# Attention's products with the values: from two split passes of 128 columns to plain fp32 at two places of 64 columns

## The chip, the cores and the metric

The kernel runs on one core of a Trainium2 chip. Its five engines work side by side, each through its own queue in order: the tensor engine (PE, with the loads of its weights shown as PEld), the vector engine (DVE), the scalar engine (ACT), GpSimd (POOL) and SyncE (SP), which issues most transfers. The metric is the device time of one execution in microseconds; the median of three runs counts.

## What is computed

One inference step of a decoder layer for a prompt of 1024 tokens and 8 single tokens ("samples") that share the weights: a half-step feed-forward block, one input projection, an attention part with 8 heads (MLA) beside an mLSTM part with 4 heads, one output projection, a second feed-forward block, a per-layer embedding and a final norm, all in fp32. The change is in the attention of the prompt, which the reference writes as follows:

```python
k_nope = (ckv @ w_uk).reshape(B, S, H, NOPE_DIM)
v = (ckv @ w_uv).reshape(B, S, H, V_DIM)          # V_DIM = 64
...
s = (jnp.einsum('bqhd,bkhd->bhqk', qn_b, k_nope, ...)
     + jnp.einsum('bqhr,bkr->bhqk', qr_b, krope, ...)) * scale
s = jnp.where(kpos[None, :] <= qpos[:, None], s, -jnp.inf)
p = jax.nn.softmax(s, axis=-1)
return jnp.einsum('bhqk,bkhd->bqhd', p.astype(v.dtype), v)
```

## The kernel before

Activations lie with features on the 128 partitions and tokens along the free axis. Most products are made of three passes in the type fp32r: operands are split into a high part (a cast on ACT) and a low part (a subtraction of that cast on DVE or GpSimd), and high x high, high x low and low x high are added in PSUM (`split` L177, `mm3` L195 to L198).

The attention of the prompt runs over 16 items: 8 heads, each with two halves of 512 queries (`Q` = 0, 1). Two generators share the loop at L1362. `scores` (L1312, `att_s` L1144) makes, for one block of 128 queries at a time, the scores of all keys up to it (`pss`, three fp32r passes of up to 512 columns for each 512 keys, L1164 to L1166), the maximum on DVE (L1168, L1171), the exponential on ACT (L1176) and the normalisation by the sum on DVE or ACT (L1183, L1181); the result is a tile `P` with queries on partitions. It runs `LEAD` = 3 blocks ahead of the other generator, `att_pv` (L1187).

`att_pv` goes over key blocks of 128 keys, 4 of them for Q = 0 and 8 for Q = 1. For a key block, `tr` transposes the blocks of `P` (up to four, one for each query block, L1196) into a PSUM tile `pT`, and splits it into an fp32r tile `PT`, one buffer for each key block: cast on ACT (L178), subtraction on DVE (L182). Three key blocks later (`SKEW`) follow two passes into `po` (L1211): the weights are 128 columns of the value tile `vv`, high halves of 64 values beside low halves, and the moving operand is the high and then the low part of `PT`, up to 512 queries wide; the last four key blocks lie on the diagonal, where 384, 256 and 128 columns are left. Rows 0 to 63 of `po` hold what the high values give, rows 64 to 127 what the low values give; a copy on ACT (L1216) and an addition on DVE (L1217) bring them together in `aT`. The value tiles come from `v_all` (L964), eight of them, each split from PSUM by ACT and DVE (L974).

Between these units stand, at places fixed by the emitted microseconds of tensor work, steps of other generators: the attention of the samples over gathered cache pages (`ss` L1072 and `ol` L1118, plain fp32 products with 32 weight columns at four places of the array; the pages `kt` and `nt` come by indirect transfers from GpSimd's queue, L1049 and L1058), the projection of the embeddings (`pj`), and near the end the preparation of the output projection (`mx`, `hT`).

The order on PE and SP is the order in the source. The order on ACT, DVE and GpSimd is set by a scheduler when the program is built, and so is which of the 43 big buffers a tile gets. `PT`, `vv`, `P`, `kt`, `nt` and the weights all share these 43 buffers, and an instruction that fills one waits for the last reader of the tile that lay there.

Of the kernel before, what the change touches and what calls it, by code (L numbers as in the profile page):

```python
# [7 lines left out]
F32 = mybir.dt.float32  # L8
F32R = mybir.dt.float32r
I32 = mybir.dt.int32  # L10
AF = mybir.ActivationFunctionType
ALU = mybir.AluOpType
# [14 lines left out]
HEADS = 8  # L27
# [26 lines left out]
ACT_NORM = (1, 3, 5)  # L54
SKEW = 3
LEAD = 3
AHEAD = 4
# [33 lines left out]
class Emitter:  # L91
    """Orders what is emitted: a step can be put off until some microseconds of tensor work lie before it,
    and slow chains are taken step by step between the units of tensor work."""

# [37 lines left out]
def trunk(ctx: ExitStack, tc, I, O):  # L132
    nc = tc.nc
    pe, act, dve, pool, sp = nc.tensor, nc.scalar, nc.vector, nc.gpsimd, nc.sync
# [12 lines left out]
    def nm(p):  # L147
        uid[0] += 1
        return f"{p}_{uid[0]}"

    def B(shape, dt=F32, p="b"):
        t = big.tile(shape, dt, tag="b", name=nm(p))
        return t
# [9 lines left out]
    def TN(shape, dt=F32, p="t"):  # L163
        t = tin.tile(shape, dt, tag="t", name=nm(p))
        return t

    def PS(shape, p="ps"):
        t = psp.tile(shape, F32, tag="ps", name=nm(p))
        return t
# [7 lines left out]
    def split(hi, lo, src, eng=None):  # L177
        act.copy(hi, src)  # L178
        if eng is pool:
            pool.tensor_tensor(out=lo, in0=src, in1=hi.bitcast(F32), op=ALU.subtract)  # L180
        else:
            dve.tensor_tensor(out=lo, in0=src, in1=hi.bitcast(F32), op=ALU.subtract)  # L182
# [23 lines left out]
    class Acts:  # L206
        """Eight feature tiles, split, cut by token group: 15 of a group's 16 slices in five tiles of its own."""

# [74 lines left out]
    class Norm:  # L283
# [6 lines left out]
        def lift(self, g, k):  # L290
            """The group's slice k times its gain only: the group's scale is left to what follows the products."""
            x = SC(p="xf")
            dve.tensor_scalar(out=x, in0=self.h[k][:, GS[g]], scalar1=gc[:, self.g0 + k:self.g0 + k + 1], scalar2=None, op0=ALU.mult)
            hi, lo = self.x.outs(g, k, 1)[0]
            split(hi, lo, x, pool if k in LIFT_POOL else None)
# [13 lines left out]

    # the units of work of one weight tile over the token groups; the last group comes late at first  # L310
    def units(n, early):
# [7 lines left out]
    def ffn(h, nrm, wg, wu, wd, nxt, order, begin, mid, ahead, lat, aheads, late={}):  # L319
        """order: the first units; the last group's second half of the norm is put in after the first unit."""  # L320
        xn = nrm.x
# [99 lines left out]

    # ---- start
    ones = C([128, 128], name="ones")
# [3 lines left out]
    h = [B([128, T], F32, "h") for _ in range(KD)]  # L427
# [46 lines left out]

    # ---- constants of the mixing part
    ident = C([128, 128], name="ident")
# [12 lines left out]
    first = [(0, 0), (1, 0), (0, 1), (1, 1), (0, 2), (1, 2)]  # L489
# [15 lines left out]

    # ---- input projection
    zs = {}
# [42 lines left out]

    # ---- gates: rows of (head, chunk), the running maximum over the chunks, columns by a transpose
    def log_sigmoid(t, rows, n):
# [21 lines left out]
    def gates():  # L574
# [3 lines left out]
        for i in range(2):  # L578
            rows = slice(64 + 32 * i, 64 + 32 * i + MH)
# [49 lines left out]
        pool.dma_start(out=acb, in_=md3.partition_broadcast(128))  # L629
        # samples  # L630
        gs = TN([MH, 2, NB_S], p="gs")
# [19 lines left out]
        pool.dma_start(out=sgb, in_=sgd.partition_broadcast(128))  # L651
        # rotary key
        trig = B([64, T], F32, "trig")
# [11 lines left out]

    # ---- mLSTM of the prompt, a chunk a step
    xd = tc.dram_tile([MH, 128, NC, CH], F32, name="xd")
# [87 lines left out]

    # ---- norms of the latents
    cks = C([128, 2, NB_S], name="cks")
# [14 lines left out]

    # ---- one step of the mLSTM for the samples, a head at a time
    xs = C([128, MH * NB_S], name="xs")
# [61 lines left out]
    for n, (i, g) in enumerate(us):  # L836
# [3 lines left out]
        if n == 3:  # L840
            spill_h()
            h = None
# [3 lines left out]
        if i > 6 and g == 2 and i % 4 == 1 and i < 21:  # L846
            hd = (i - 9) // 4
# [14 lines left out]

    # ---- MLA projections, kept in DRAM until their head's turn
    vd = tc.dram_tile([8, 128, HEADS * 128], F32, name="vtd")
# [99 lines left out]
    def v_all(uvh, uvl):  # L964
        for kb in range(8):
            ps = PS([128, 512])
            t = slice(kb * 128, (kb + 1) * 128)
            for ct in range(2):
                mm3(ps, ck[ct][0][:, t], ck[ct][1][:, t], uvh[:, ct, :], uvl[:, ct, :], ct == 0, ct == 1)
            vv = B([128, HEADS, 128], F32R, "vv")  # L970
            split(vv[:, :, 0:64], vv[:, :, 64:128], ps.rearrange("p (h v) -> p h v", h=HEADS))
            vtok.append(vv)
            em.spend(1.3)
            yield  # L974
# [10 lines left out]
    vtok = []  # L985
# [29 lines left out]

    # ---- attention of the samples over their pages
    NI = NB_S * N_PAGES
# [8 lines left out]
    aT = [B([128, T], F32, "aT") for _ in range(4)]  # L1026
# [113 lines left out]

    # ---- attention of the prompt
    em.flush()
# [44 lines left out]
    def att_pv(hd, P, Q):  # L1187
        po = PS([128, 512], "po")
        nkb = 4 * Q + 4
        pxs = {}  # L1190

        def tr(kb):
            j0 = max(0, kb - 4 * Q)
            ps = PS([128, 4, 128], "pT")
            for j in range(j0, 4):
                pe.transpose(ps[:, j, :], P[j][:, kb * 128:(kb + 1) * 128], ident)  # L1196
            px = B([128, 2, 4, 128], F32R, "PT")
            split(px[:, 0, j0:4, :], px[:, 1, j0:4, :], ps[:, j0:4, :])
            pxs[kb] = px

        for kb in range(SKEW):
            tr(kb)
            yield
        for kb in range(nkb):
            if kb + SKEW < nkb:
                tr(kb + SKEW)
            yield
            j0 = max(0, kb - 4 * Q)
            px = pxs.pop(kb)
            for i in range(2):  # L1210
                pe.matmul(po[:, j0 * 128:512], vtok[kb][:, hd, :], px[:, i, j0:4, :].rearrange("p j q -> p (j q)"),  # L1211
                          start=(kb == 0 and i == 0), stop=(kb == nkb - 1 and i == 1))
            px = None
        r0 = 64 * (hd % 2)
        t = aT[hd // 2][r0:r0 + 64, 512 * Q:512 * Q + 512]
        act.copy(t, po[0:64])  # L1216
        dve.tensor_tensor(out=t, in0=po[64:128], in1=t, op=ALU.add)  # L1217
        yield
# [56 lines left out]

    # ---- output projection of the mixing part
    n2 = Norm(None, "xn", G_FF2)
    wo = {}

    h = []  # L1280
# [46 lines left out]
    for i in range(V_PRE):  # L1327
        next(vs, None)
    while done < 4 + LEAD:
        next(sc)  # L1330
# [31 lines left out]
    for n, (hd, Q) in enumerate(items):  # L1362
        pv = att_pv(hd, Ps.pop(n), Q)
        steps = SKEW + 1 + 4 * Q + 4
        left = len(items) - 1 - n
        for i, _ in enumerate(pv):
            em.spend(0.6)
            at(left, i)
            while done < 4 * (n + 1) + LEAD + 4 * (i + 1) / steps:
                next(sc)  # L1370
# [18 lines left out]
    aT = None  # L1389
# [30 lines left out]

    # ---- per-layer embedding and the final norm
    def ple_unit(m, g):
# [31 lines left out]
    fin, last, pjs = {}, {}, []  # L1454
# [136 lines left out]
```

## Time and profile before

| | |
|---|---|
| median of three runs | 2379.93 us (2379.78 to 2381.81) |
| span of the profiled execution | 2381.1 us |
| PE, PEld busy | 2294.8, 2220.7 us |
| DVE, ACT, GpSimd busy | 1084.0, 732.8, 416.5 us |
| attention of the prompt, about 1157 to 1417 us | 260 us |

The page gives the profiled execution by its span, which lies within the spread of the three runs. Busy time of PE is counted from a matmul's start to its modelled end, and matmuls overlap, so the lengths that matter are those from one start to the next. The clock of the tensor engine has two levels, 1.2 and 2.4 GHz; the profile gives the granted share, 1.00 or 0.50, or the mean of a stretch. In a view of waits a row names the engine that waited, the line, and who ended the wait.

### The profile page before, as it was taken

The page shows a single profiled execution, that of the slowest core. Times are in us where ns is not written, and L with a number is a line of the kernel's source. Part 1 is how long each engine was busy: PE and PEld are TensorE (multiplying, and loading weights), DVE is VectorE, ACT ScalarE, POOL GpSimd, SP SyncE. Part 2 cuts the span into 40 slices and gives each one's busy share as a digit, 9 for nine tenths or more (in the row PEclk, how much of TensorE's full clock was granted, in tenths as well). Part 3 has the DMA queues.
Part 4 walks back from the last instruction along what each step waited for, and adds up shares of the span by engine and source line. Part 5 has one row for each costly group of instructions (what it writes and reads, how often), then busy time and mean ns, then how long its engine had stood idle before and what let it go on. Part 6 is the DMA issues. An engine that isn't in the chain of part 4 may idle for free.

```text
span 2381.1 us, 35330 instructions
## 1 busy us (share of the span) xinstructions
PE 2294.8 (96%) x14479; PEld 2220.7 (93%) x14479; DVE 1084.0 (46%) x2231; ACT 732.8 (31%) x1496; POOL 416.5 (17%) x403
## 2 busy tenths in 40 slices
PE   8999999999998999999888889999999999999997
PEld 7999999999998999999666679999999999999996
DVE  7332332333335656447766677623223223223575
ACT  5211211202213334444655553411121120211353
POOL 4101101101103321102565314200000000000233
PEclk9999999999999999999989989999999999999998
DMA  3111011120121313224964530111111112112213
GB/s 134 38 52 60 29 55 54 32 75 28 43 75 59 109 48 93 82 86 165 260 164 134 160 136 28 45 38 52 55 33 54 56 32 70 33 38 78 62 38 107
DMA packets 77883, 177.84 MB, mean 75 GB/s; under 512 B 11200, under 2 KB 37408, under 8 KB 77720
## 3 DMA queue, kind: packets, MB, share of 16 engines
q1 hardware_dynamic: 67432, 153.22, 21.1%
q0 software_dynamic: 6832, 18.12, 2.9%
q10 hardware_dynamic: 3456, 4.23, 0.6%
q8 instruction: 114, 1.87, 0.3%
q14 instruction: 49, 0.40, 0.1%
HBM read 146.58 MB, written 28.95 MB: 74 GB/s over the span
## 4 chain that ended last, share of the span: by engine, by line
PE 82%; DVE 9%; DMA 4%; ACT 3%; issue 2%; POOL 1%; SPq 0%; ACTq 0%; DVEq 0%; POOLq 0%
PE pd L197 7%; PE pd L198 7%; PE pd L196 7%; PE pg L198 7%; PE pu L197 7%; PE pu L196 7%; PE pu L198 7%; PE pg L197 7%; PE pg L196 7%; PE pz L197 3%; PE pz L196 3%; PE pz L198 3%; DVE xf L279 2%; PE po L1211 1%; DMA kt<-in_cT,idx_t 1%
## 5 line engine op out<-in xcount | busy, mean ns | idle before, releaser
L196 PE MATMUL pd<-hdh,wh 128*128 128x344 f32 x1056 | 341.0, 323 | 5.8 <-ACT hdh L178 5.8
L197 PE MATMUL pd<-hdl,wh 128*128 128x344 f32 x1056 | 340.0, 322 | 3.4 <-DVE hdl L182 3.3
L197 PE MATMUL pg<-xn,wh 128*128 128x344 f32 x1056 | 338.6, 321 | 4.5 <-DVE xn L182 3.8
L198 PE MATMUL pd<-hdh,wl 128*128 128x344 f32 x1056 | 339.7, 322 | 0.0
L196 PE MATMUL pg<-xn,wh 128*128 128x344 f32 x1056 | 338.1, 320 | 0.9 <-ACT xn L178 0.9
L196 PE MATMUL pu<-xn,wh 128*128 128x344 f32 x1056 | 338.5, 321 | 0.3 <-DVE si L347 0.3
L198 PE MATMUL pu<-xn,wl 128*128 128x344 f32 x1056 | 337.8, 320 | 0.8 <-DVE wl L182 0.8
L198 PE MATMUL pg<-xn,wl 128*128 128x344 f32 x1056 | 337.9, 320 | 0.5 <-DVE wl L182 0.3
L197 PE MATMUL pu<-xn,wh 128*128 128x344 f32 x1056 | 337.9, 320 | 0.0
L178 ACT CAST wh<-wr 128x1024 fp32r<-128x1024 f32 (+2 forms) x195 | 180.4, 935 | 371.8 <-PE pd L197 291.2
L182 DVE TENSOR_TENSOR wl<-wr,wh 128x1024 fp32r<-128x1024 f32 (+2 forms) x195 | 215.5, 1105 | 116.3 <-ACT wh L178 111.5
L353 DVE TENSOR_TENSOR hp<-si,pu 128x344 f32<-128x344 f32 x132 | 67.7, 513 | 420.5 <-PE pu L198 413.0
L365 DVE SCALAR_TENSOR_TENSOR h<-pd,h 128x344 f32<-128x344 f32 x240 | 123.2, 515 | 280.1 <-PE pd L198 280.1
L254 POOL TENSOR_TENSOR sq<-sq,sq 128x344 f32<-128x344 f32 x66 | 70.6, 1070 | 798.6 <-ACT sq L249 770.7
L196 PEld LDWEIGHTS pd<-hdh,wh 128*128 128x128 f32 x1056 | 200.0, 189 | 7.1 <-ACT hdh L178 6.7
L197 PEld LDWEIGHTS pg<-xn,wh 128*128 128x128 f32 x1056 | 198.7, 188 | 6.4 <-DVE xn L182 5.2
L197 PEld LDWEIGHTS pd<-hdl,wh 128*128 128x128 f32 x1056 | 200.0, 189 | 4.6 <-DVE hdl L182 4.2
L198 PEld LDWEIGHTS pd<-hdh,wl 128*128 128x128 f32 x1056 | 200.0, 189 | 0.0
L196 PEld LDWEIGHTS pg<-xn,wh 128*128 128x128 f32 x1056 | 198.6, 188 | 1.5 <-ACT xn L178 1.2
L198 PEld LDWEIGHTS pg<-xn,wl 128*128 128x128 f32 x1056 | 198.7, 188 | 1.1 <-DVE wl L182 1.1
L198 PEld LDWEIGHTS pu<-xn,wl 128*128 128x128 f32 x1056 | 198.6, 188 | 1.1 <-DVE wl L182 1.1
L196 PEld LDWEIGHTS pu<-xn,wh 128*128 128x128 f32 x1056 | 198.6, 188 | 1.0 <-issue 0.8
(384 smaller groups left out, 4174.9 us busy)
## 6 DMA issues: line engine op xcount, KB each, us to landing
wr<-in_wu SPq DMA_DIRECT2D x44, 512.0 KB, 3.6
wr<-in_wg SPq DMA_DIRECT2D x43, 512.0 KB, 3.7
wr<-in_wd SPq DMA_DIRECT2D x64, 320.0 KB, 2.9
wr<-in_w_in SPq DMA_DIRECT2D x22, 512.0 KB, 3.8
h<-in_xT SPq DMA_DIRECT2D x24, 172.0 KB, 4.2
hsp<-h SPq DMA_DIRECT2D x8, 516.0 KB, 3.4
ppd<-pj SPq DMA_DIRECT2D x24, 172.0 KB, 2.2
h<-hsp SPq DMA_DIRECT2D x8, 516.0 KB, 5.9
```

Source lines behind the costliest of these rows:

```text
L178: act.copy(hi, src)
L182: dve.tensor_tensor(out=lo, in0=src, in1=hi.bitcast(F32), op=ALU.subtract)
L196: pe.matmul(ps, whi, xhi, start=first, stop=False)
L197: pe.matmul(ps, whi, xlo, start=False, stop=False)
L198: pe.matmul(ps, wlo, xhi, start=False, stop=last)
L254: pool.tensor_tensor(out=acc[0], in0=acc[0], in1=q, op=ALU.add)
L279: dve.scalar_tensor_tensor(out=x, in0=s[:, c], scalar=gc[:, g0 + k:g0 + k + 1], in1=r, op0=ALU.mult, op1=ALU.mult)
L353: dve.tensor_tensor(out=p, in0=s, in1=pu, op=ALU.mult)
L365: dve.scalar_tensor_tensor(out=h[m][:, c], in0=pd, scalar=0.5, in1=h[m][:, c], op0=ALU.mult, op1=ALU.add)
L1211: pe.matmul(po[:, j0 * 128:512], vtok[kb][:, hd, :], px[:, i, j0:4, :].rearrange("p j q -> p (j q)"), start=(kb == 0 and i == 0), stop=(kb ...
```

## The change

- The value tiles are no longer split. `v_all` copies the PSUM tile to plain fp32 on DVE; two key blocks share one buffer, so there are four value tiles in place of eight.
- `tr` no longer splits. The transposed probabilities are copied in plain fp32, on DVE for even key blocks and on ACT for odd ones; two key blocks share one buffer `PT`. The four query blocks lie at positions 0, 2, 3, 1.
- The products are plain fp32. The weights are the 64 values of the head. Positions 0 and 1 (query blocks 0 and 3) go to rows 0 to 63 of `po`, positions 2 and 3 (query blocks 1 and 2) to rows 64 to 127, each 256 columns wide, 128 on the diagonal, none for the second place in the last key block: 15 or 7 products for an item in place of 16 or 8 passes. `po` has 256 columns in place of 512.
- At the end two copies on ACT bring `po` to `aT`; the addition on DVE is gone.

```diff
+PV_POS = (0, 2, 3, 1)
+PV_LIVE = ((0, 0), (1, 0), (1, 1), (1, 2))
...
-            vv = B([128, HEADS, 128], F32R, "vv")
-            split(vv[:, :, 0:64], vv[:, :, 64:128], ps.rearrange("p (h v) -> p h v", h=HEADS))
-            vtok.append(vv)
+            if kb % 2 == 0:
+                vv = B([128, 2, HEADS * 64], F32, "vv")
+            dve.tensor_copy(vv[:, kb % 2], ps)
+            vtok.append(vv[:, kb % 2])
...
-        po = PS([128, 512], "po")
+        po = PS([128, 256], "po")
...
-                pe.transpose(ps[:, j, :], P[j][:, kb * 128:(kb + 1) * 128], ident)
-            px = B([128, 2, 4, 128], F32R, "PT")
-            split(px[:, 0, j0:4, :], px[:, 1, j0:4, :], ps[:, j0:4, :])
+                pe.transpose(ps[:, PV_POS[j], :], P[j][:, kb * 128:(kb + 1) * 128], ident)
+            if kb % 2 == 0:
+                pts[:] = [B([128, 2, 4, 128], F32, "PT")]
+            px = pts[0][:, kb % 2]
+            live = (slice(0, 4), slice(1, 4), slice(1, 4, 2), slice(1, 2))[j0]
+            if kb % 2 == 0:
+                dve.tensor_copy(px[:, live, :], ps[:, live, :])
+            else:
+                act.copy(px[:, live, :], ps[:, live, :])
...
-            for i in range(2):
-                pe.matmul(po[:, j0 * 128:512], vtok[kb][:, hd, :], px[:, i, j0:4, :].rearrange("p j q -> p (j q)"),
-                          start=(kb == 0 and i == 0), stop=(kb == nkb - 1 and i == 1))
+            v = vtok[kb][:, 64 * hd:64 * hd + 64]
+            for i, p0 in enumerate(PV_LIVE[j0]):
+                if p0 < 2:
+                    pe.matmul(po[64 * i:64 * i + 64, p0 * 128:256], v, px[:, 2 * i + p0:2 * i + 2, :].rearrange("p j q -> p (j q)"),
+                              start=kb == 0, stop=kb == nkb - 1 - i)
...
-        act.copy(t, po[0:64])
-        dve.tensor_tensor(out=t, in0=po[64:128], in1=t, op=ALU.add)
+        act.copy(t[:, 0:4:3, :], po[0:64].rearrange("p (j q) -> p j q", j=2))
+        act.copy(t[:, 1:3, :], po[64:128].rearrange("p (j q) -> p j q", j=2))
```

How this stands in the built program, in one of the halves with 8 key blocks. On the tensor engine before (L1211 are the passes with the values, L1196 the transposes):

```order
L1211 MATMUL po_12087<-PT_12093,vv_10628 128x512 x2
L1196 MATMUL pT_12208<-ident,P_11823 128x128
L1196 MATMUL pT_12208<-ident,P_11880 128x128
L1196 MATMUL pT_12208<-ident,P_11923 128x128
L1196 MATMUL pT_12208<-ident,P_11973 128x128
L1211 MATMUL po_12087<-PT_12122,vv_10651 128x512 x2
L1196 MATMUL pT_12218<-ident,P_11880 128x128
```

On the tensor engine after the change, at the same place (its lines are numbered by the new file, L1224 and L1201):

```order
L1224 MATMUL po_12008<-PT_12014,vv_10628 64x256 x2
L1201 MATMUL pT_12123<-ident,P_11758 128x128
L1201 MATMUL pT_12123<-ident,P_11811 128x128
L1201 MATMUL pT_12123<-ident,P_11852 128x128
L1201 MATMUL pT_12123<-ident,P_11900 128x128
L1224 MATMUL po_12008<-PT_12014,vv_10628 64x256 x2
L1201 MATMUL pT_12132<-ident,P_11811 128x128
```

No matmul has moved against another; each pair of full passes with 128 output rows is a pair of products with 64 output rows, and two successive pairs read one buffer.

On the vector engine before, at the same place (L182 are the subtractions, L1168 to L1183 the softmax of the blocks ahead):

```order
L182 TENSOR_TENSOR PT_12093<-pT_12088,PT_12093 128x512
L1168 ISA pss_12107,nmx_12106<-pss_12107,mask_qk 128x512
L1168 ISA nmx_12106 128x1
L1173 TENSOR_SCALAR nmx_12106<-nmx_12106 128x1
L182 TENSOR_TENSOR PT_12122<-pT_12117,PT_12122 128x512
L182 TENSOR_TENSOR PT_12130<-pT_12125,PT_12130 128x512
L1179 RECIPROCAL sm_12113<-sm_12113 128x1
L182 TENSOR_TENSOR PT_12138<-pT_12133,PT_12138 128x512
```

On the vector engine after the change:

```order
L1207 COPY PT_12014<-pT_12009 128x512
L1182 RECIPROCAL sm_12000<-sm_12000 128x1
L1186 TENSOR_SCALAR P_11991<-P_11991,sm_12000 128x384
L1171 ISA pss_12027,nmx_12026<-pss_12027,mask_qk 128x512
L1171 ISA nmx_12026 128x1
L1176 TENSOR_SCALAR nmx_12026<-nmx_12026 128x1
L1207 COPY PT_12048<-pT_12043 128x512
L1182 RECIPROCAL sm_12033<-sm_12033 128x1
```

Four subtractions have become two copies, and the normalisation of `P` stands behind the first copy where it stood ahead of the first subtraction; the other two copies are on the scalar engine's queue in the place of two of its four casts.

## Rows read from the trace of the kernel before

**Rows 1.** The page's slices: granted clock in 40 equal slices of the span

```profile
PEclk9999999999999999999989989999999999999998
```

**Rows 2.** Stretches: length, PE, PEld, DVE, ACT, POOL busy, PEclk, DMA share, GB/s

```profile
1157.00:1417.00 260.00, 220.16 (x1390) 170.30 (x1389) 176.78 (x519) 153.88 (x400) 123.48 (x129) 0.89 0.58 159
1166.20:1176.40 10.20, 7.94 (x36) 5.27 (x37) 4.41 (x15) 3.12 (x11) 7.76 (x9) 0.50 0.86 208
...
1244.70:1251.50 6.80, 5.75 (x19) 4.65 (x20) 1.93 (x5) 0.58 (x1) 3.64 (x4) 0.50 0.76 208
1251.50:1299.00 47.50, 43.61 (x299) 33.84 (x299) 33.87 (x108) 29.97 (x84) 21.97 (x24) 1.00 0.46 130
```

**Rows 3.** Waits of matmuls, 1157 to 1417: us in total, times, longest

```profile
PE ss L1072 <- DMA kt<-in_cT,idx_t: 7.0, 7, 2.8
PE ol L1118 <- DMA nt<-in_cN,idx_n: 6.3, 3, 2.5
PE po L1211 <- DVE PT L182: 6.1, 11, 1.1
PE pT L1196 <- DVE PT L182: 5.9, 1, 5.9
...
PE po L1211 <- ACT PT L178: 2.1, 5, 0.5
```

**Rows 4.** Waits of the weight loads, the same stretch

```profile
PEld po L1211 <- DVE PT L182: 9.6, 14, 1.5
PEld ol L1118 <- DMA nt<-in_cN,idx_n: 7.9, 4, 3.0
PEld pT L1196 <- DVE PT L182: 6.8, 2, 6.4
```

**Rows 5.** Timeline of matmuls: start us, length us, line, operation, tiles, count

```profile
1350.17 0.72 PE L1211 MATMUL po<-PT,vv 128*128 128x512 f32 x2
1350.73 0.49 PE L1196 MATMUL pT<-ident,P 128*128 128x128 f32 x3
```

**Rows 6.** Timeline of matmuls around two steps of the samples' attention

```profile
1273.73 1.04 PE L1196 MATMUL pT<-ident,P 128*128 128x128 f32 x8
1274.70 1.50 PE L1072 MATMUL ss<-kt,qz 96*32 96x256 f32 x24
1276.13 0.50 PE L1164 MATMUL pss<-kTh,qTh 96*128 96x512 f32 x1
1276.46 0.39 PE L1165 MATMUL pss<-kTl,qTh 96*128 96x512 f32 x1
1276.69 0.40 PE L1166 MATMUL pss<-kTh,qTl 96*128 96x512 f32 x1
...
1354.87 1.07 PE L1118 MATMUL ol<-nt,spT 128*32 128x256 f32 x16
1355.87 0.44 PE L1211 MATMUL po<-PT,vv 128*128 128x384 f32 x1
```

**Rows 7.** Timeline: two `ss` products alone, first passes, then all four

```profile
1165.28 0.41 PE L1072 MATMUL ss<-kt,qz 96*32 96x256 f32 x2
...
1165.28 0.63 PE L1072 MATMUL ss<-kt,qz 96*32 96x256 f32 x4
```

**Rows 8.** Groups by shape: count, busy us, mean ns, idle before and releasers

```profile
L182 DVE TENSOR_TENSOR PT<-pT,PT 128x512 fp32r<-128x512 f32 x48 | 32.2, 684 | 6.0 <-ACT PT L178 5.6
L178 ACT CAST PT<-pT 128x512 fp32r<-128x512 f32 x48 | 27.2, 589 | 10.4 <-PE pT L1196 10.4
L1217 DVE TENSOR_TENSOR aT<-po,aT 64x512 f32<-64x512 f32 x16 | 11.1, 694 | 1.0 <-ACT aT L1216 0.2
```

**Rows 9.** Timeline: a gather on GpSimd, and the tensor engine at two places

```profile
1209.06 0.94 POOL L1058 DMA_INDIRECT nt<-in_cN,idx_n  x1 [7.73 <-PE po L1211]
...
1199.73 0.63 PE L1166 MATMUL pss<-kTh,qTl 96*128 96x512 f32 x1
...
1245.75 1.06 PE L1118 MATMUL ol<-nt,spT 128*32 128x256 f32 x2 [2.54 <-DMA nt<-in_cN,idx_n]
```

More of the change, by code (lines that the diff above doesn't have):

```diff
@@ L1187, in att_pv @@
     def att_pv(hd, P, Q):
-        po = PS([128, 512], "po")
+        po = PS([128, 256], "po")
         nkb = 4 * Q + 4
         pxs = {}
+        pts = []
         def tr(kb):
@@ L1209, in att_pv @@
             px = pxs.pop(kb)
-            for i in range(2):
-                pe.matmul(po[:, j0 * 128:512], vtok[kb][:, hd, :], px[:, i, j0:4, :].rearrange("p j q -> p (j q)"),
-                          start=(kb == 0 and i == 0), stop=(kb == nkb - 1 and i == 1))
+            v = vtok[kb][:, 64 * hd:64 * hd + 64]
[3 more added lines that the diff above has]
+                              start=kb == 0, stop=kb == nkb - 1 - i)
             px = None
         r0 = 64 * (hd % 2)
-        t = aT[hd // 2][r0:r0 + 64, 512 * Q:512 * Q + 512]
-        act.copy(t, po[0:64])
-        dve.tensor_tensor(out=t, in0=po[64:128], in1=t, op=ALU.add)
+        t = aT[hd // 2][r0:r0 + 64, 512 * Q:512 * Q + 512].rearrange("p (j q) -> p j q", j=4)
+        act.copy(t[:, 0:4:3, :], po[0:64].rearrange("p (j q) -> p j q", j=2))
+        act.copy(t[:, 1:3, :], po[64:128].rearrange("p (j q) -> p j q", j=2))
+        pts.clear()
         yield
```

## Prediction

> **What bounds the kernel now.** I read the views from coarse to fine. The page's row of the granted clock [rows 1] says where to look: the array's clock is full nearly everywhere, except in slices 19 to 24, and these are the attention of the prompt, 1157 to 1417 us. Nothing outside that stretch is touched by the change but the projection of the values just before it. Of the 260 us of this stretch the matmul engine is busy 220, the vector engine 177, the scalar engine 154, and the mean granted clock is 0.89 [rows 2]. With two levels, 2.4 and 1.2 GHz, a mean of 0.89 means 0.22 x 260 = 57 us at the low one, in which matmuls take twice as long: about 29 us lost.
>
> So the stage is the tensor engine's, with holes. The waits name them. By the matmul rows [rows 3], 14.1 us go to transposed probabilities (`po` and a transpose waiting for DVE `PT` 6.1 and 5.9, `po` for ACT `PT` 2.1), 13.3 us to gathered cache pages (`ss` 7.0, `ol` 6.3), and about 12 to other things. Those rows count the array's run-out as busy, so they are low. The weight loader's rows are high: 9.6 + 6.8 for DVE `PT` alone, 7.9 for `ol` [rows 4]. I take values between: 17 us for `PT`, 15 us for gathers. The clock falls behind such holes: after the `ol` products waited 2.5 us until 1245.75 [rows 9], 1244.7 to 1251.5 ran at 0.50 [rows 2].
>
> **Price on the tensor engine.** Now, each key block takes two passes of 512 columns (fewer on the diagonal). From the first pass's start to the next transpose is 0.56 us [rows 5], of which 0.11 is the first load of weights in place of the last transpose's own slot; the passes themselves are 0.23 each, as the scores' passes of 512 columns show (1276.46 to 1276.69 [rows 6]). An old visit of one full block is worth 2 x 0.23 = 0.465 us.
>
> After the change a visit is two products of 64 weight columns and 256 columns, in plain fp32, which the trace records as two passes each. The kernel before has no such product with 64 columns at two places, but it has `ss` and `ol`: plain fp32, 256 columns, weights of 32 columns at four places. 24 passes of `ss` take 1.43 us from the first start to the next product's start (1274.70 to 1276.13), 16 passes of `ol` take 1.00 (1354.87 to 1355.87) [rows 6]. The difference is 0.43 for two rounds of four passes: a round costs 0.215 us however many places run in it, and 0.14 us are fixed. Before them, eight transposes and the start of `ss` take 0.97 us (1273.73 to 1274.70), where eight transposes are 0.88 at 0.11 each (eight last 1.04 in all and three 0.49 [rows 5, 6]): 0.09 to empty the array first. Behind them the next product's first pass takes 0.33 in place of 0.23 [rows 6]: 0.10, because its weights could not be loaded early; in front of a transpose I take 0.06, between 0 and this 0.10. Weights of 64 columns in place of 32 add 0.03 (an estimate: a transpose that must load 128 columns takes 0.11). A visit thus has 0.32 us of border in front of a transpose and 0.36 in front of anything else, and a full block costs two rounds, 0.43, against 0.465.
>
> In the program's order there are 75 visits before and after, at the same places, and nothing else on this engine has moved. 43 are a lone full block: 43 x (0.32 + 0.43 - 0.465) = 12.3 us. Eight are a lone last block of 128 columns (two short rounds, 0.21, against 0.17): 2.9. 24 hold blocks of the diagonal, where one place has 128 columns and the other 256 and the round is as long as the longer: a block of 384 columns costs 0.32 + 0.43 against 2 x 0.175, +0.40, one of 256 followed by one of 128 costs 0.32 + 0.43 against 0.41, +0.34 (old passes taken at 0.23 x columns / 512, at least 0.06 each and 0.11 for the last): 24 x 0.37 = 8.9. 32 visits stand in front of something else than a transpose: 1.3. Twelve borders exist already, where `ss`, `ol` or `sn` stand beside a visit: -1.4. Sum 24.0 at full clock, 25 with the share of the stage at half clock. This price is all on the path; nothing hides it but the holes.
>
> The count of two rounds rests on one more row. Of two `ss` products that stood alone, the first two passes started together at 1165.28, and all four had ended 0.63 us later [rows 7]: two rounds of 0.215 and the run-out (0.41 - 0.215 = 0.195) make 0.625, three would make 0.84. A rule of the Trainium skill speaks for three: "TensorE: Matmul & The Clock Gate", Part 3, The mechanism, says that matmuls start and end strictly in program order even across places, by which place 0's second pass would hold up place 1's first. The trace does not bear it out for passes of fp32, and the sum goes by the trace.
>
> **What is taken away.** The split is two steps in a row: ACT casts (0.589 us for 512 columns), then DVE subtracts from it (0.684) [rows 8]. 96 of each become 48 plain copies on DVE (even key blocks) and 48 on ACT (odd ones). A DVE copy is not in this shape in the trace; the subtraction, 0.684, bounds it from above, and I charge that. DVE loses the 32.2 us of its 48 subtractions of 512 columns, some 20 in 48 shorter ones, and 11.1 in the 16 final additions [rows 8]; it gets 32 copies of 512 and 16 of 256 columns, at most 28 us: some 35 less of 177. ACT loses 27.2 and some 18 and gets 22, and a second final copy, +3: some 20 less of 154. Neither counts as time by itself. What counts is that a block's products wait for one engine after the transposes, no longer for two, and that each queue is shorter. Against about 0.6 us less latency stand 16 holes before `po` of 0.5 us each, the longest 1.1 [rows 3]. I take two thirds of 17: -11 us, rounded up to -12 because the 5.9 us hole before a transpose stands behind the final mixing's casts and splits on DVE, where the new program has a copy on each of two engines. Bounds: 0 and -17.
>
> Buffers: a pair of blocks shares one buffer, where each had its own, and the eight value tiles become four. The gathers on GpSimd's queue need such buffers: one stood 7.7 us until 1209.06 for `po` to give one back [rows 9]. In the new program that gather waits for a scores product that runs at 1199.73 [rows 9], before the queue gets there; of the other gathers that waited for `po`, most wait there for an earlier instruction too. So they come up to 8 us sooner, while the tensor engine comes later by its price. Of 15 us about 3 lie at the very first gathers (before 1171) and stay; of the other 12 I take -10. Bounds: 0 and -12.
>
> Clock: 10 us of the 57 at half clock (1166 to 1176 [rows 2]) follow those first gathers and stay. If half of the other 47 go with the holes, 23 us of half clock give back 12. Bounds: +5, should the emptied borders let the clock fall more often, and -22.
>
> The values' projection swaps cast and subtraction for a copy; no wait stands there. The final mixing, the scores and all transfers keep their work.
>
> Sum: +25 - 12 - 10 - 12 = -9 us. Made against the profiled span of 2381.1, which is 0.05% over the median of 2379.9; on the median it gives **2371 us**.
>
> **The rivals.** (A) *The array is simply full, and slower.* The borders are paid 75 times, while the holes only shift: DVE and ACT are ordered anew by the scheduler, and a copy that is stuck behind a normalisation on its queue holds a block up as a split did. Then only 10 us of holes come back and no clock: 2380 + 25 - 10 = 2395. It decides as soon as holes and clock return less than 25 us. For it: 12 us of holes have nothing to do with splits or gathers. Against it: DVE loses a fifth of its work.
> (B) *Even.* The same with 20 to 29 us back: 2375 to 2385.
> (C) *The places don't run abreast*, so the change doesn't do what it says. If a product's second pass holds up the other place, 64 blocks take three long rounds and 16 three short ones: 64 x 0.215 + 16 x 0.107 = 15 more, 2386; if everything goes in a row, 48 x 0.43 + 32 x 0.215 = 28 more, 2399. This is the skill's strict order of above. [rows 6, 7] speak against it; 64-wide places were not seen.
> (D) *The holes go and the clock stays up*: -17 - 12 - 22 + 25 = -26, 2354. For it: the clock held at 1.00 from 1251.5 to 1299 [rows 2], where the matmul engine was busy 43.6 of 47.5 us.
>
> **How the numbers follow.** 0.2% is 4.8 us, about what a measurement of this kernel can tell from no change: faster below 2375, slower above 2385. Forecast 0.43, D 0.15, B 0.19, A 0.16, C 0.07. Faster: forecast and D, 0.58; same 0.19; slower: A and C, 0.23. The range must leave out no more than 0.2: from D's 2354 to A's 2395.
>
> **What would show it.** Right: a lone visit of four passes takes 0.57 to 0.62 us from first start to next start; `PT` as a releaser of `po` falls below 6 us; the GpSimd rows lose the waits for `po`; the stage's mean clock rises above 0.93 and its length falls from 260 to about 251. Wrong: visits of 0.8 us or more (C); waits for `PT` or `P` as long as before (A); more of the stage at half clock though its holes are shorter.

## The result, and the profile after

The changed kernel takes 2362.24 us (2359.39 to 2364.27); beside it the kernel before took 2379.86 us. The ratio is 0.9923, 95% interval 0.9909 to 0.9937: 17.6 us or 0.77% less. The prediction was 2371, within 2354 to 2395: the direction was right, the gain twice as large as forecast. Beside the last experiments the changed kernel gave 0.9937 (0.9925 to 0.9949), so that 15 to 18 us is a fair reading.

The profiled execution of the changed kernel has a span of 2362.5 us, 18.6 less than before. The stage starts at the same time; its last product with the values starts at 1396.15 us, where it was 1414.58. So all of the gain lies in the attention of the prompt. I read the views in the order of the prediction: first the stretch that answers to the first line of [rows 2] (length, PE, PEld, DVE, ACT and GpSimd busy, mean granted clock, DMA share, GB/s), which the shorter stage ends at 1398.40:

```profile
1157.00:1398.40 241.40, 221.96 (x1553) 153.14 (x1552) 149.03 (x453) 136.48 (x366) 123.42 (x128) 0.91 0.65 175
```

The stretch is 18.6 us shorter, while PE is busy as long as before. DVE has lost 28 us of work, ACT 17. The mean granted clock rose from 0.89 only to 0.91: 0.18 x 241 = 43 us at the low level, where 57 were. What the matmuls wait for (us in total, times, longest), against [rows 3]:

```profile
PE ss L1075 <- DMA kt<-in_cT,idx_t: 8.9, 4, 4.5
PE pT L1201 <- ACT PT L1209: 2.5, 1, 2.5
PE ol L1121 <- DMA nt<-in_cN,idx_n: 2.2, 1, 2.2
...
PE po L1224 <- DVE PT L1207: 1.5, 1, 1.5
```

The 14.1 us for `PT` are 4.0 now. The gathers are still there: 11.1 us in five long waits, where 13.3 were in ten; `ss` has even more than before.

A visit of the array is seen in the timeline of matmuls (start, length, line, operation, tiles, count), here in a window that opens on the first two passes and in one that holds all four:

```profile
1275.40 0.44 PE L1224 MATMUL po<-PT,vv 128*64 128x256 f32 x2
...
1275.40 0.65 PE L1224 MATMUL po<-PT,vv 128*64 128x256 f32 x4
1275.98 0.33 PE L1201 MATMUL pT<-ident,P 128*128 128x128 f32 x1
```

Two passes, one at each place, start together at 1275.40, and the next transpose starts 0.583 us after them. That is two rounds of 0.215 and 0.15 of border. Before them the array empties: from the last transpose's start to the visit's start it is 0.20 us (0.26 in some), where a transpose alone takes 0.11. Behind them one more piece of border follows. A later window shows the start of the second transpose behind the visit; the last line is the same transpose behind a visit in the kernel before, where the first one started at 1350.73 [rows 5]:

```profile
1276.15 0.38 PE L1201 MATMUL pT<-ident,P 128*128 128x128 f32 x2
...
1350.84 0.38 PE L1196 MATMUL pT<-ident,P 128*128 128x128 f32 x2
```

The second two passes start at 1275.67, 0.267 us after the first, so that 0.05 of the 0.15 lies between the rounds and 0.10 behind the second. The first transpose behind the visit then holds the array for 0.165 us, where it was 0.108 in the kernel before.

Last, the copies of 512 columns on DVE (count, busy us, mean ns, idle before):

```profile
L1207 DVE COPY PT<-pT 128x512 f32<-128x512 f32 x32 | 22.0, 687 | 6.0 <-PE pT L1201 5.8
```

The copy on DVE takes 687 ns, as long as the subtraction that it replaces, 684 [rows 8].

**The stage divided by starts.** The waits count a run-out as busy, so for the comparisons below I divided each trace in another way. Every interval from one matmul's start to the next is held against the usual interval of the same two shapes at full clock, doubled where the granted clock is 0.50. What lies more than 0.15 us above is a hole, put down to the product that came late. The table is worked out from the traces and rough: taken again with other usual intervals and with limits from 0.15 down to 0.03 us, the difference between the two kernels is 19 to 22 us at full clock, -34 to -36 in the holes and -3 to -4 at half clock, and single columns move by up to 13 (`ss`, `ol` before). It reaches from the first scores product (about 1144 us) to the end of the last product with the values. "At full clock" is what the tensor engine would need without holes, "half clock" what the low level added.

| kernel | stage | at full clock | half clock | holes | of them `po` | `pT` | `ss`, `ol` | rest |
|---|---|---|---|---|---|---|---|---|
| before | 270.1 | 192.4 | 22.5 | 55.2 | 15.8 | 8.8 | 19.6 | 11.0 |
| changed | 251.9 | 209.1 | 17.4 | 25.4 | 3.1 | 2.8 | 13.8 | 5.7 |
| difference | -18.2 | +16.7 | -5.1 | -29.8 | -12.7 | -6.0 | -5.8 | -5.3 |

A second profile of the changed kernel (beside the last experiments) divides as 250.1 = 208.5 + 16.4 + 25.2. So the tensor engine has 17 to 22 us more work, and 35 to 40 us of holes and low clock are gone. Which part of the change did that is not in the table; the experiments ask for it.

### The profile page after: what moved, and what is told of

Same layout as the page of the kernel before. It is cut to its first block, busy times and chain, and to the rows that moved or that the text cites. A ratio compares the mean times of both kernels' runs of the same rounds, so it can differ in the third digit from the quotient of the medians.

```text
span 2362.5 us, 35504 instructions
## 1 busy us (share of the span) xinstructions
PE 2296.3 (97%) x14639; PEld 2202.9 (93%) x14639; DVE 1057.6 (45%) x2167; ACT 713.3 (30%) x1456; POOL 416.2 (18%) x403
## 4 chain that ended last, share of the span: by engine, by line
PE 84%; DVE 8%; ACT 3%; DMA 3%; issue 1%; POOL 1%; SPq 0%; ACTq 0%; DVEq 0%; POOLq 0%
PE pd L199 7%; PE pd L200 7%; PE pd L198 7%; PE pg L200 7%; PE pu L198 7%; PE pu L199 7%; PE pg L199 7%; PE pu L200 7%; PE pg L198 7%; PE pz L199 3%; PE pz L198 3%; PE pz L200 3%; DVE xf L281 2%; PE po L1224 2%; PE pT L1201 1%
```

## The experiments

The change is made of four parts: other **products**, **one step** in place of two for each block of `PT`, two blocks in one **`PT` buffer**, two value tiles in one **value buffer**. The first experiments undo or do them one at a time.

**The two steps put back into the changed kernel.**

```diff
-            if kb % 2 == 0:
-                dve.tensor_copy(px[:, live, :], ps[:, live, :])
-            else:
-                act.copy(px[:, live, :], ps[:, live, :])
+            act.copy(px[:, live, :], ps[:, live, :])
+            dve.tensor_tensor(out=px[:, live, :], in0=ps[:, live, :], in1=px[:, live, :], op=ALU.max)
```

> The changed kernel with one part undone: each block of transposed probabilities is again made in two steps in a row, a copy on ACT and then an operation on DVE that reads the same PSUM tile and the copy (a maximum, which leaves the values as they are), as cast and subtraction were. Products, buffers and final copies stay as in the changed kernel. Theory (the chain of two engines made the holes before the products): the holes before `po` and before the late transpose, about 19 us by the starts of the matmuls in the two traces, come back, with some 5 us of half clock: 2380 to 2388. Rival (the gain came from the buffers and the gathers; the products would have found the copies ready either way): within 0.2% of the changed kernel, 2357 to 2367.

Measured: 2375.6 us, ratio 0.9990 (0.9977 to 1.0003), 13 to 16 us above the changed kernel, so the rival falls. The sum of the theory was some 5 to 12 us too high: the holes before `po` came back only from 3.1 to 7.2 us and those before `pT` from 2.8 to 6.1, while the holes before `ss` and `ol` shrank from 13.8 to 11.2.

**Own buffers in the changed kernel**, for `PT` and for the value tiles, and then for the value tiles alone.

```diff
-            if kb % 2 == 0:
-                pts[:] = [B([128, 2, 4, 128], F32, "PT")]
-            px = pts[0][:, kb % 2]
+            px = B([128, 4, 128], F32, "PT")
...
-            if kb % 2 == 0:
-                vv = B([128, 2, HEADS * 64], F32, "vv")
-            dve.tensor_copy(vv[:, kb % 2], ps)
+            vv = B([128, HEADS * 64], F32, "vv")
+            dve.tensor_copy(vv, ps)
```

> The changed kernel with another part undone: each key block has a buffer `PT` of its own again, and each of the eight value tiles one of its own; copies and products stay. Theory of the prediction (the shared buffers let the gathers start sooner, worth 10 us of holes and their clock): 2372 to 2377, with the waits of GpSimd for `po` back. Rival (the gathers came sooner by little of their own account: holes before `ss` and `ol` fell only from about 19 to 13 us, and the rest of the gain has nothing to do with buffers): 2357 to 2367.

> The changed kernel with each of the eight value tiles in a buffer of its own again, the transposed probabilities sharing theirs as in the change. It divides the 11 us that own buffers for both cost. Theory (the four value buffers are free for the whole stage, the `PT` pairs only for moments): most of the 11 us come back, 2369 to 2374. Rival (the gathers take the buffers that `PT` leaves, and the value tiles are only a number of buffers): 2360 to 2366.

Measured: 2373.4 us with own buffers for both, ratio 0.9979 (0.9969 to 0.9990), and 2363.5 us with own value buffers alone, 0.9928 (0.9915 to 0.9942). So in the changed kernel the buffers are worth 10 to 11 us, as forecast, and all of it is in `PT`; the value tiles give nothing, which was the rival of the second run. The waits of GpSimd with own buffers for both are of the kind of before:

```profile
POOL nt L1060 <- PE po L1221: 9.5, 2, 7.9
```

In the changed kernel no gather waits for `po`. By the sums of the waits and holes the forecast's mechanism (gathers that come sooner) would not be borne out: with own value buffers alone the gathers wait as badly (`kt` 12.1 us for `po`, `nt` 11.5 for `pT`), and the holes before `ss` and `ol` are 20.5 us against 19.4 with own buffers for both. The order in time shows it all the same. With own buffers for both, the 41st gather, the one of [rows 9], waits for `po`, and the `ol` products that need the pages behind it wait in their turn:

```profile
1208.67 1.15 POOL L1060 DMA_INDIRECT nt<-in_cN,idx_n  x1 [7.93 <-PE po L1221]
...
1241.99 0.62 PE L1120 MATMUL ol<-nt,spT 128*32 128x256 f32 x2 [1.57 <-DMA nt<-in_cN,idx_n]
...
1244.88 0.62 PE L1120 MATMUL ol<-nt,spT 128*32 128x256 f32 x2 [2.28 <-DMA nt<-in_cN,idx_n]
```

With shared `PT` buffers and own value buffers the same gather starts 5.2 us sooner, all that follow it come 5 to 10 us sooner, and the 16 passes run without a wait:

```profile
1203.47 0.94 POOL L1060 DMA_INDIRECT nt<-in_cN,idx_n  x1 [0.59 <-DVE pel L184]
...
1240.41 1.07 PE L1120 MATMUL ol<-nt,spT 128*32 128x256 f32 x16
```

At 1237 us the kernel with shared buffers is 1 us behind; from 1252 us on it is 5.6 us ahead, and at the end of the stage 5.2, which is the whole difference of the two traces. In between it loses 4.5 us at a later wait of `ss` and gains 3 again, which is why the sums hide it. The two traces differ by 5 us only, so the rest of the 10 is not accounted for.

**One cast in the kernel before**: the chain of the change without its products; and the same with shared `PT` buffers.

```diff
-            split(px[:, 0, j0:4, :], px[:, 1, j0:4, :], ps[:, j0:4, :])
+            if kb % 2 == 0:
+                dve.tensor_copy(px[:, 0, j0:4, :], ps[:, j0:4, :])
+            else:
+                act.copy(px[:, 0, j0:4, :], ps[:, j0:4, :])
...
-                pe.matmul(po[:, j0 * 128:512], vtok[kb][:, hd, :], px[:, i, j0:4, :].rearrange("p j q -> p (j q)"),
+                pe.matmul(po[:, j0 * 128:512], vtok[kb][:, hd, :], px[:, 0, j0:4, :].rearrange("p j q -> p (j q)"),
```

> The kernel before with the low part of the transposed probabilities left out: one cast per key block, on DVE for even and on ACT for odd blocks, and both passes read the high part, so that the tensor engine has every pass that it had. This is the change's chain without its price on the tensor engine, and with the buffers and the final addition of before. Theory (the price is real and lies on the path; by the starts of the matmuls a lone visit takes 0.785 us from the last transpose's start to the next one's, against 0.576 before, 17 us over all visits): 17 us below the changed kernel, 2340 to 2350; by the 25 us of the prediction 2337. Rival (the borders fill time that the engine would have waited anyway): 2357 to 2367.

> The kernel before with one cast per key block (the low part of the transposed probabilities is left out, both passes read the high part) and, unlike the run with one cast before it, two key blocks in one buffer `PT`; the eight value tiles stay, split. It has the same buffers as the next run, and only the products, the value tiles' making and the final addition differ, so the two together give the price of the new products once more. Theory (price 16 to 17 us, as between the runs with own buffers): 16 us below the next run, about 2350 to 2356. Rival (the price shrinks where holes would have been): less than 8 us below the next run.

Measured: 2357.3 us with own buffers, ratio 0.9910 (0.9895 to 0.9924), and 2357.7 us with shared ones, 0.9903 (0.9888 to 0.9918). One step in place of two is worth 22 us in the kernel before; it is the largest part. Both theories on the price were off. The first run lands at the edge of its rival's range; it is 16 us below the changed kernel with own buffers, which has the same chain, but only 5 below the changed kernel; the second is 6 us below its partner. So the rival of the second is right: the price shrinks where holes would have been. At full clock the two pairs differ by as much as the table says (192.9 against 211.8, and 192.5 against 209.9), but the faster tensor engine runs into the gathers: the second run has 23.1 us of holes before `ss` and `ol`, its partner 20.5. The two runs also show what shared `PT` buffers are worth here: nothing, though the 41st gather starts at 1202.0 us in place of 1207.6. So the 10 us that they give in the changed kernel are not theirs alone.

**The new products alone**, with two steps and own buffers.

> The kernel before with the new products alone: plain fp32 at two places, but each key block has its own buffer `PT`, each value tile its own, and each block is made in two steps in a row, a copy on ACT and an operation on DVE that reads the same PSUM tile and the copy, as cast and subtraction were. (The final addition on DVE is a second copy on ACT, as in the change.) Theory (the price is 16 us of the array, all on the path): 2390 to 2397, 2395 being the first rival of the prediction. Rival (the holes before the gathers' products, which stand at fixed times of GpSimd's queue, take up a part of the price, as between the two runs that share `PT`, where 17 us more of products cost 6): 2382 to 2388.

Measured: 2387.6 us, ratio 1.0034 (1.0021 to 1.0047): 8 to 9 us slower than before, and so the second of the two theories. The waits show that the products wait for `PT` about as long as before (7.3 us, [rows 3] has 6.1 and 2.1); the long wait of a transpose is not there:

```profile
PE po L1219 <- DVE PT L1204: 7.3, 6, 1.8
PE ss L1074 <- DMA kt<-in_cT,idx_t: 4.2, 5, 2.1
PE ol L1120 <- DMA nt<-in_cN,idx_n: 3.2, 2, 2.2
```

and that a later tensor engine waits less for the pages: 7.4 us, where [rows 3] has 13.3. With this run the parts can be put on one after another:

| from | to | part added | median, us | step |
|---|---|---|---|---|
| before | products alone | products | 2387.6 | +8 to +9 |
| products alone | own buffers | one step | 2373.4 | -13 to -14 |
| own buffers | own value buffers | `PT` buffers | 2363.5 | -10 to -12 |
| own value buffers | changed | value buffers | 2362.2, 2362.9 | about 0 |

| kernel | stage | at full clock | half clock | holes | `po` | `pT` | `ss`, `ol` | rest |
|---|---|---|---|---|---|---|---|---|
| products alone | 276.4 | 208.1 | 27.2 | 41.1 | 11.6 | 8.0 | 11.8 | 9.7 |
| own buffers | 260.8 | 211.8 | 15.8 | 33.3 | 2.4 | 4.1 | 19.4 | 7.4 |
| own value buffers | 254.8 | 209.9 | 12.2 | 32.8 | 2.9 | 2.8 | 20.5 | 6.6 |

The step from two to one takes 13 us of holes before `po` and `pT` and 11 us of low clock, and gives 8 us back before the gathers' products. The order matters: one step alone, put on first, gave 22.

**All copies on DVE.**

```diff
-            if kb % 2 == 0:
-                dve.tensor_copy(px[:, live, :], ps[:, live, :])
-            else:
-                act.copy(px[:, live, :], ps[:, live, :])
+            dve.tensor_copy(px[:, live, :], ps[:, live, :])
```

> The changed kernel with all copies of the transposed probabilities on DVE, none on ACT. The chain to the products is one step, as in the change, but DVE has 96 copies in place of 48, some 27 us more work, and ACT as much less. Theory (what counts is one step in place of two in a row, not the load of a queue): 2360 to 2368. Rival (DVE's queue of copies and softmax is what the products waited for): the holes before `po` come back, 2372 or more.

> The changed kernel itself, beside the other runs on one chip. Both theories: 2357 to 2367, a ratio of 0.991 to 0.994 to the kernel before.

Measured: 2363.1 us, ratio 0.9933 (0.9920 to 0.9946), beside the changed kernel's 2362.9, 0.9937 (0.9925 to 0.9949). 48 copies more on DVE cost nothing, though DVE does

```profile
L1206 DVE COPY PT<-pT 128x512 f32<-128x512 f32 x48 | 32.2, 684 | 6.3 <-PE pT L1201 5.8 <-issue 0.3
```

where the changed kernel has 32 of this shape. So a longer queue on DVE is not what the products waited for. Each block's way can be followed in the traces, from the end of its last transpose to the end of its last copy, as a mean of the 96 blocks: 3.1 us with the two steps put back, 1.3 in the changed kernel, 1.5 with all copies on DVE. Of the 1.8 us that the two steps cost, the second step and the wait for its engine make 1.24 (0.69 and 0.55); 0.57 is a longer wait until the first step starts on ACT, which then has 96 of these copies in its queue, not 48. No run has all 96 copies on ACT alone, so how much of the loss is the second step and how much ACT's queue is not shown.

**The products of two key blocks in one visit**, in the changed kernel.

```diff
-            px = pxs.pop(kb)
...
+            for b in (kb - 1, kb) if kb % 2 else ():
+                px = pxs.pop(b)
```

> The changed kernel with the products of two key blocks in one visit, after the odd one: 47 visits of the array in place of 75, the same products, and the even block's products come one step later. Theory (each visit has a border of about 0.25 us, of which the trace shows 0.09 before it and 0.15 behind its two rounds): 28 x 0.25 = 7 us less, 2355. Rival (the longer visits only make the engines behind them wait longer, or the border is not saved since the rounds do not close up): 2360 or more.

Measured: 2355.9 us, ratio 0.9907 (0.9893 to 0.9922), 4 to 7 us less than the changed kernel. A visit of eight passes in this kernel's timeline:

```profile
1273.71 1.08 PE L1224 MATMUL po<-PT,vv 128*64 128x256 f32 x8
1274.72 0.33 PE L1201 MATMUL pT<-ident,P 128*128 128x128 f32 x1
```

From start to next start it is 1.01 us: four rounds of 0.215 and the same 0.15. So the border is paid by the visit, not by the product. The stage needs 201.0 us at full clock in place of 209.1, 8.1 less for 28 visits less: 0.29 each, which agrees with 0.09 in front, 0.15 and the 0.06 of the transpose behind, 0.30.

**The gathers sooner**, in the changed kernel and in the one with pairs.

```diff
-SA_E, SA_D = 4.5, 14.0
+SA_E, SA_D = 4.5, 9.5
...
-                kts = nxt
-                nxt = load_t(bt, pp + 1) if pp < 3 else None
+                kts = kq.pop(0)
...
+                kts = None
+                if pp < 2:
+                    kq.append(load_t(bt, pp + 2))
+                else:
+                    nn += [load_n(bt, 2 * pp - 4), load_n(bt, 2 * pp - 3)]
...
-            nn = [load_n(bt, 0), load_n(bt, 1)]
...
-                if pg < 6:
-                    nn.append(load_n(bt, pg + 2))
-                elif pg == 6 and bt == 0:
-                    nxt = load_t(1, 0)
+                if pg < 4:
+                    nn.append(load_n(bt, pg + 4))
+                elif pg % 2 and bt == 0:
+                    kq.append(load_t(1, pg // 2 - 2))
```

> The changed kernel with the gathers issued sooner in the program: the first ones one step earlier, the pages for the products `ss` two steps ahead in place of one, those for `ol` four tiles ahead in place of two, and the second group's first two sets during the `ol` steps of the first. Theory (the holes before `ss` and `ol` that are left, 11.4 and 2.4 us by the starts of the matmuls, are late gathers): half to two thirds of them go, with their share of half clock: 2350 to 2356. Rival (GpSimd issues a gather each 1.2 us, 64 in a row, and the buffers are no sooner free; the holes move to the next gather, or `P` and `PT` now wait for buffers): 2360 or more.

> The products of two key blocks in one visit, as in the run with pairs, and the gathers sooner, as in the run before this one. Theory (border and holes are separate costs): the two gains add up, some 6.5 + 8 below the changed kernel, 2345 to 2350. Rival (the time won on the tensor engine makes the gathers late again): 2354 or more.

Measured: 2350.0 us, ratio 0.9869 (0.9854 to 0.9884), and with pairs 2341.9 us, 0.9839 (0.9826 to 0.9852). The waits of the first for pages (the rows of `ol` are gone):

```profile
PE ss L1077 <- DMA kt<-in_cT,idx_t: 3.0, 5, 1.1
```

The holes before `ss` and `ol` fell from 13.8 to 5.9 us. The stage of the version with both, in the columns of [rows 2]:

```profile
1157.00:1376.23 219.23, 204.71 (x1533) 147.76 (x1532) 145.75 (x448) 134.77 (x363) 125.01 (x128) 0.94 0.70 191
```

The two gains add up, and this version is 38 us (1.6%) faster than the kernel before and 20 faster than the changed one. The granted clock stands at 0.94.

## Why the prediction was right, and by what it missed

**What bounds.** Right: the whole difference lies in the stage that was named, and its starts and holes carry it.

**The price on the tensor engine: +25, measured 17 to 22.** The test on a visit was met: 0.57 to 0.62 was asked for and 0.583 came. The places run abreast, in two rounds, so (C) falls. It is seen best where the places differ in width: in the visit at 1222.79 us a pass of 128 columns and one of 256 start 0.007 us apart, and their second passes 0.160 and 0.273 us after the first start. The strict order across places that the Trainium skill states for matmuls ("TensorE: Matmul & The Clock Gate", Part 3, The mechanism) agrees with the trace for each product as a whole, since the second one starts and ends 0.007 us after the first. For the passes of plain fp32 it does not hold: the second place's first pass starts ahead of the first place's second, and three rounds would make 0.80 us.

The border, taken at 0.32 us, measures 0.30: 0.09 in front, as forecast, 0.05 between the rounds, 0.10 behind, and 0.06 by which the first transpose's slot grows. From the last transpose's start to that of the second one behind it, a lone full visit takes 0.684 us before and 0.951 after: 0.27 more, where the sum had 0.285. A lone last block costs 0.31 in place of 0.36, a diagonal visit of 256 and 128 columns 0.29 in place of 0.34, the ones with 384 some 0.36 to 0.41 in place of 0.40. So by the visits the price is 43 x 0.27 + 8 x 0.31 + 24 x 0.35 + 1.3 - 1.4 = 22 us (an estimate, its last two terms as in the sum), where the sum had 24. The table's 17 is lower; it counts every wait below 0.15 us as work.

That this price lies on the path in full was wrong. Alone it made the kernel 8 to 9 us slower; by the tables 14 us of holes went against it, 8 of them before the gathers' products, while low clock added 5. The gathers keep their times (with the products alone they start within 1.6 us of before, up to the 97th of 128), and a slower tensor engine meets them later. The prediction had put all cover of this kind at nothing.

**The holes before `PT`: -12, measured -19.** By the waits they fell from 14.1 to 4.0 us, by the starts the holes before `po` and `pT` fell from 24.6 to 5.9. The upper bound of 17 was nearer than the two thirds that I took; the 5.9 us wait before a late transpose fell to 2.5. (Of the 19, some 4 are waits for `P` and its maximum, not for `PT`: 4.5 us before, 0.3 after, by the waits.) That the change from two steps to one brings this is shown by the run that puts the second step back and by the one with one cast. Of the other half of the reason, shorter queues, the run with all copies on DVE shows that DVE's queue had no part; ACT's is not separated from the step.

**The gathers: -10, measured -2 by the waits and -6 by the starts.** The first link was right: the gather that stood until 1209.06 us [rows 9] starts at 1202.43 in the changed kernel and does not wait for `po` any more, and those behind it start 6 to 16 us sooner than before.

The runs with own buffers show the second link too, at the `ol` products at 1240 us. What the sum missed is that a tensor engine that comes sooner waits again at the next gathers: the waits before `ss` grew from 7.0 to 8.9 us. The size, 10 us for the `PT` buffers in the changed kernel, is partly luck, since the same buffers gave nothing in the kernel with one cast.

**The clock: -12, measured -5.** 14 of the 57 us at half clock went, where 23 were forecast, and the mean of 0.93 that was asked for was not reached. Of the 44 us that are left, 27 follow or hold the waits of `ss` and `ol` (1166 to 1180, 1241 to 1245, 1296 to 1306). The other 17 do not: 1204 to 1210 follows waits before the projection `pj`, 1384 to 1391 follows the transpose that waited 2.5 us, and 3 us at 1265 follow no hole above 0.4 us. Two of the first kind:

```profile
1165.50:1180.00 14.50, 11.37 (x51) 6.52 (x49) 4.52 (x17) 3.62 (x13) 9.84 (x12) 0.53 1.04 229
...
1240.00:1246.00 6.00, 4.84 (x20) 3.52 (x22) 1.23 (x4) 0.58 (x1) 2.50 (x3) 0.72 0.87 221
```

**What the sum left out: -5.** Short holes before the scores and other products, 11.0 before and 5.7 after, were taken as fixed.

Together, by the table: 17 - 19 - 6 - 5 - 5 = -18, against +25 - 12 - 10 - 12 = -9. The price came out 8 us lower than forecast, `PT` 7 and the other holes 5 better, the gathers 4 and the clock 7 worse. If the price is 22, as by the visits, the holes gave back as much more. The direction and the mechanism of the copies were right; that errors of 4 to 8 us in most terms left the number within its range is partly luck.

**The rivals.** (A) had 2395, the full price with 10 us of holes back. The products alone are the nearest run and gave 2388: the sign was right, the size 7 us too high. (D) had 2354, with a clock that stays up; the changed kernel lies between it and the forecast. With the gathers sooner the same products take 2350.0 us, below (D), though the mean clock rises only to 0.93 (0.94 with pairs too). So the products don't rule (D)'s time out; the late gathers were a large part of what kept the changed kernel from it, and the clock gave less than (D) had.

## What to carry to other kernels

Price a product that switches the array's places by the visit: two rounds for plain fp32 with the places abreast, and 0.30 us of border however many products stand in the visit; then put as many into one as the data allow. A second engine in the chain ahead of a product, with the longer queue that it brought, cost 13 to 22 us here, and its wait (0.69 us for a block) was as long as its work (0.55). A price on a full engine is partly paid by holes that another engine's pace sets, so that gains and prices measured alone don't add up: here one part gave 22 us when put on first and 13 to 14 when put on second, and another gave 10 to 12 in one kernel and nothing in the other.

## What was not expected of the hardware

- A copy from PSUM on DVE, 512 columns of plain fp32, takes 684 to 687 ns, and the subtraction of a second operand in SBUF took 684 [rows 8]: the second operand was free.
- The border from a visit's first start to the next product's start is the same for four passes of 256 columns (0.583 - 2 x 0.215 = 0.15) and for eight (1.01 - 4 x 0.215 = 0.15), and nearly so for 64 weight columns at two places as for 32 at four (0.14 [rows 6]). The product behind pays 0.06 to 0.10 more.
- GpSimd's indirect gathers follow one another at 1.2 us at best, 0.92 busy and 0.30 between, so a set of eight takes 10 us. In the version with pairs and sooner gathers, for instance:

```profile
1151.33 0.93 POOL L1038 DMA_INDIRECT kt<-in_cT,idx_t  x1 [0.30 <-issue]
1152.56 0.91 POOL L1038 DMA_INDIRECT kt<-in_cT,idx_t  x1 [0.30 <-issue]
```
